# A two-layer transformer trunk on one core: weights repacked by the host, x also loaded transposed, and a first chunk that keeps the weights in the array

## The chip, the core and the metric

The kernel runs on one core of a Trainium2 chip. The metric is the device time of one launch in microseconds (us), the median of several runs. TensorE (PE) multiplies, VectorE (DVE) and ScalarE (ACT) do the elementwise work, GpSimd (POOL) a few small jobs, and SyncE (SP) issues all transfers (DMAs) in one queue, in program order.

## What is computed

The reference is a decoder trunk of two layers over 256 tokens of width 1024, in float32. Each layer is: half a SwiGLU feed-forward step, attention, a second half step, and a gated input embedding, each followed by a layer norm of `sqrt(2) * x + step`. Layer 0 has "forgetting" attention with 16 heads, layer 1 latent attention (MLA) with 16 heads.

```python
def swiglu(x, w_in, w_out):
    h = x @ w_in                                  # 1024 -> 2 * 2816
    gate, up = h[..., :D_FF], h[..., D_FF:]
    return (jax.nn.silu(gate) * up) @ w_out       # 2816 -> 1024

x = post_norm(x, 0.5 * swiglu(x, ffn1_w_in[i], ffn1_w_out[i]), ln_g[i, 0], ln_b[i, 0])
x = post_norm(x, mix, ln_g[i, 1], ln_b[i, 1])     # mix: FoX (i = 0) or MLA (i = 1)
x = post_norm(x, 0.5 * swiglu(x, ffn2_w_in[i], ffn2_w_out[i]), ln_g[i, 2], ln_b[i, 2])
gate = jax.nn.sigmoid(x @ ple_w_gate[i] + ple_b_gate[i])
x = post_norm(x, gate * (p[i] @ ple_w_proj[i]), ln_g[i, 3], ln_b[i, 3])
```

## The kernel before, in words

**Split products.** Every float32 operand of a matmul is split into two parts in a shorter format: `hi`, a copy rounded by ACT, and `lo = value - hi`, made by DVE (lines 194 and 195 for weights, 522 and 523 for activations). A product is three matmuls: hi·hi, hi·lo, lo·hi. So every weight passes from HBM into a `raw` buffer (1 MB, three of them), is split by ACT and DVE in *units* of 128 x 1024 into a slot of `hl` (ten slots, and up to four borrowed buffers called `ota`, `otb`, `qk`, `fs`), and is then used by TensorE.

**The stream.** `Stream` knows the order of all weights from a dry run. A *group* is one `raw` buffer, two units. `load` issues the next group's DMAs on SP as soon as the program has split an earlier group, so that at most three groups are in flight; SP then waits, in order, until the buffer's last reader is done. `pump`, which is called between matmuls, emits the split of the next unit if a small planner (`pe_t`, `act_t`, `dve_t`, `arrives`, with an assumed 4.2 us for a group) thinks that its data are there and that ACT and DVE are not far behind. The order of ACT, DVE and PE instructions is thus fixed when the program is built.

**The feed-forward step.** The 2816 hidden columns are worked through in 11 chunks of 256 (256 gate and 256 up columns each). `HT(c)` computes a chunk transposed: the weights are stationary (128 x 128), and `xT`, the split and transposed x, moves with its 256 tokens. That is 8 k-tiles x 4 column blocks x 3 products, 96 matmuls of 256 columns. `W` multiplies the chunk's result with its `w_out` rows.

**The first chunk of the program** (`first`, used with `cold=True` for ffn1 of layer 0) is different, as nothing has been loaded yet. x comes in eight DMAs of 128 KB (two token tiles by four column quarters), interleaved with sixteen 128 KB DMAs of the first two weight groups (`between`, lines 338 to 350, in `loads`; `fine` is 1 for these groups, 2 for the third and 4 from then on). `turn(t, q)` transposes two 128 x 128 tiles of x on TensorE (line 517) and splits the result into `xT`. `part(t, k, w)` then has x stationary and the weights moving: three matmuls of 512 columns for each token tile and k-tile, 48 in all. `act` forms `silu(gate) * up` for one token tile, and `T(0)`, later, transposes the result in four steps. Ahead of all this `setup` and `first` run `spin(2)` (line 493): two float32 matmuls of the all-zero `mask` each, whose results nobody reads. Between them `mask` gets its triangles from POOL (line 482).

Chunk 1 (`HT(1)`) follows at once with `T(0)` between its second and third unit, then chunks 2, 3 and 4 and their `W` steps.

Of the kernel before, what the change touches and what calls it, by code (L numbers as in the profile page):

```python
# [16 lines left out]
DFF = 2816  # L17
# [14 lines left out]
FINE = 4  # L32
# [59 lines left out]
class Recorder:  # L92
# [10 lines left out]
    lend = reclaim = check = load = busy = pair = split = ahead = later = split_now = fill = pump  # L103
# [3 lines left out]
class Stream:  # L107
# [66 lines left out]
    def split(self, between=lambda: None, half=False):  # L174
# [18 lines left out]
        def part(c):  # L193
            nc.scalar.activation(hi[:, c], src[:, c], AF.Copy)  # L194
            nc.vector.tensor_tensor(lo[:, c], src[:, c], hi[:, c].bitcast(F32), op=ALU.subtract)  # L195

        if self.ready < FINE:
            self.hl[key] = w
            part(slice(0, 1))
            between()  # L200
            part(slice(1, 2))
        elif key[0] == "pb":
            nc.gpsimd.memset(w[:, 0, :].bitcast(F32), 0.0)
            lo = w[32:33, 0, :n]
            part(slice(None))
        elif half:
            nc.scalar.activation(hi, src, AF.Copy)
            self.busy(act=n)

            def rest():  # L210
                nc.vector.tensor_tensor(lo, src, hi.bitcast(F32), op=ALU.subtract)
                self.busy(dve=n)
                self.split_done(key, w)

            self.rest = rest
            return
        else:
            part(slice(None))
# [113 lines left out]
def make_loads(a):  # L332
    def rows(ap, k0, n):
        return ap[k0 * 128 : (k0 + n) * 128, :].rearrange("(k p) c -> p k c", p=128)

    def loads(q, g, raw, fine, between):
        k, i = g[0], g[-1]
        if k == "win":
            w = a[g[2]][0][g[1]]
            c = g[3]  # L340
            r = raw.rearrange("p (k c) -> p k c", c=512)
            n = fine
            for k0 in range(0, 4, n):
                if n == 1 and (i, k0) in between:
                    between[i, k0]()
                for s in range(2):
                    c0 = DFF * s + 256 * c
                    q.dma_start(
                        r[:, k0 : k0 + n, 256 * s : 256 * s + 256], rows(w[:, c0 : c0 + 256], 4 * i + k0, n)
                    )  # L350
        elif k == "fv":
            w = a["fox_w_in"][0]
            q.dma_start(raw.rearrange("p (k c) -> p k c", c=512), rows(w[:, 2048:2560], 4 * i, 4))
        elif k == "fvb":
            w = a["fox_w_in"][0]
            q.dma_start(raw.rearrange("p (k c) -> p k c", c=256), rows(w[:, 2560:2816], 0, 8))
        elif k == "fvc":
            w = a["fox_w_in"][0]
            n = 6 - 4 * i
            q.dma_start(raw[:, 0 : 272 * n].rearrange("p (k c) -> p k c", c=272), rows(w[:, 2816:3088], 6 * i, n))  # L360
        elif k in ("fk", "fq"):
            w = a["fox_w_in"][0]
            c = (1024 if k == "fk" else 0) + 256 * i
            q.dma_start(raw.rearrange("p (k c) -> p k c", c=256), rows(w[:, c : c + 256], 0, 8))
        elif k in ("wout", "fo", "pg", "pp", "mo"):
            if k == "wout":
                w = a[g[2]][1][g[1]]
            elif k == "fo":
                w = a["fox_w_o"][0]
            elif k == "mo":  # L370
                w = a["mla_w_o"][0]
            elif k == "pg":
                w = a["ple_w_gate"][g[1]]
            else:
                w = a["ple_w_proj"][g[1]]
            q.dma_start(raw.rearrange("p (k c) -> p k c", c=1024), rows(w, 2 * i, 2))
        elif k == "pb":
            q.dma_start(raw[0:1, 0:1024], a["ple_b_gate"][g[1] : g[1] + 1, :])
        elif k == "kd":
            q.dma_start(raw[:, 0:1280].rearrange("p (k c) -> p k c", c=320), rows(a["kv_w_down"], 4 * i, 4))  # L380
        elif k == "dq":
            q.dma_start(raw[:, 0:1536].rearrange("p (k c) -> p k c", c=384), rows(a["mla_w_dq"][0], 4 * i, 4))
        elif k == "qr":
            w = a["mla_w_uq"][0]
            for s in range(2):
                kk = 2 * i + s
                if kk < 3:
                    q.dma_start(
                        raw[:, 1024 * s : 1024 * s + 1024].rearrange("p (h d) -> p h d", d=64),
                        w[128 * kk : 128 * kk + 128, :, 128:192],  # L390
                    )
        elif k == "kvv":
            w = a["kv_w_up"]
            for kk in range(2):
                q.dma_start(
                    raw[:, 512 * kk : 512 * kk + 512].rearrange("p (h d) -> p h d", d=128),
                    w[128 * kk : 128 * kk + 128, 4 * i : 4 * i + 4, 128:256],
                )
        elif k == "kq":
            for kk in range(5):  # L400
                w, r = (a["kv_w_up"], kk) if kk < 2 else (a["mla_w_uq"][0], kk - 2)
                q.dma_start(
                    raw[:, 256 * kk : 256 * kk + 256].rearrange("p (h d) -> p h d", d=128),
                    w[128 * r : 128 * r + 128, 2 * i : 2 * i + 2, 0:128],
                )
        else:
            raise KeyError(g)

    return loads
# [13 lines left out]
class Trunk:  # L423
# [33 lines left out]
    def setup(self):  # L457
# [18 lines left out]
        warm = self.tl([128, 1], F32, "ss", 2)  # L476
# [10 lines left out]
        self.S.lend("ota", "otb", "qk", "fs")  # L487
# [12 lines left out]
    def load_x(self, t, q):  # L500
        c = slice(256 * q, 256 * q + 256)
        self.dma(self.x[t][:, c], None if self.rec else self.a["x"][0, 128 * t : 128 * t + 128, c])


# [99 lines left out]

    def ffn(self, li, which, lni, kv=False, ple=False, at=None, cold=False):
# [12 lines left out]
        def first():  # L618

            ps = [self.bank("h") for _ in range(2)]  # L620

            def part(t, k, w):
                for i, j in SWEEPS[4][0]:
                    self.mm(
                        ps[t], self.xT[:, t, i, k, :], w[:, j, 512 * (k % 2) : 512 * (k % 2) + 512],
                        k == 0 and (i, j) == (0, 0), k == 7 and (i, j) == SWEEPS[4][0][-1],
                    )

            def turn(t, q):
                tr = self.bank("tr")  # L630
                c = slice(2 * q, 2 * q + 2)
                for i in range(2):
                    k = 2 * q + i
                    self.transpose(tr[:, 128 * i : 128 * i + 128], self.x[t][:, 128 * k : 128 * k + 128])
                self.parts(
                    self.xT[:, t, 0, c, :], self.xT[:, t, 1, c, :],
                    tr[:, 0:256].rearrange("p (k c) -> p k c", c=128),
                )

            S.hold = True  # L640
            turn(0, 0)
            self.spin(2)
            old = None
            for u in range(4):
                key = ("win", li, which, 0, u)

                def mid():
                    turn(1, u)
                    if u:
                        part(1, 2 * u - 1, old)  # L650
                    part(0, 2 * u, S.hl.get(key, Dummy()))

                S.split(mid)
                if self.rec:
                    mid()
                w = old = self.use(key)
                if u < 3:
                    turn(0, u + 1)
                else:
                    S.split()  # L660
                part(0, 2 * u + 1, w)
                if u == 3:
                    act(0, 0, ps[0])
                    S.split()
                part(1, 2 * u, w)
            S.split()
            part(1, 7, w)
            S.hold = False
            act(0, 1, ps[1])
# [21 lines left out]
        def HT(c, what=None):  # L691
            ring = "tr" if c % 2 == cold else "h"
            ps = [self.bank(ring) for _ in range(2)]
            for u in range(4):
                if u == 1 + (cold and c == 1) and what:
                    what()
                w = self.use(("win", li, which, c, u))
                for kk, b in ((kk, b) for kk in range(2) for b in range(4)):
# [6 lines left out]
                    )  # L705
            gt = self.tl([128, 768], F32, "P", 2)[:, 0:512]
# [35 lines left out]
        def spare(ring):  # L742
            tr = self.bank(ring)
            for k in range(4):
                self.transpose(tr[:, 128 * k : 128 * k + 128], self.ident)

        turns = (
            lambda: T(0, "h"),
            lambda: spare("h") if cold else T(1, "tr"),
# [869 lines left out]
```

## Time and profile before

| what | before |
|---|---|
| time, median of 3 runs | 1083.58 us (1083.28 to 1084.54) |
| profiled execution: span, first to last instruction | 1080.8 us |
| what lies around the span, against the median | 2.8 us |
| PE, DVE, ACT busy | 1065.8, 718.8, 543.3 us |
| read from HBM | 196.35 MB, 183 GB/s over the span |
| DMA packets | 151428, of which 130994 are under 2 KB and 11954 under 512 B |

The page gives no separate time for the profiled execution; its span and the median differ by the 2.8 us that lie around it, and this document takes these as they are. In the views a row such as `L513 PE MATMUL h<-hl,xT 128*128 128x512 f32 x48` means: line 513, TensorE, a matmul into tile `h` from `hl` and `xT`, 48 of them with 512 columns. The ends of matmuls are modelled, so the mean duration of a matmul is longer than the distance from one to the next; the chain of work that ended last shows the distance.

### The profile page before, as it was taken

The page shows a single profiled execution, that of the slowest core. Times are in us where ns is not written, and L with a number is a line of the kernel's source. Part 1 is how long each engine was busy: PE and PEld are TensorE (multiplying, and loading weights), DVE is VectorE, ACT ScalarE, POOL GpSimd, SP SyncE. Part 2 cuts the span into 40 slices and gives each one's busy share as a digit, 9 for nine tenths or more (in the row PEclk, how much of TensorE's full clock was granted, in tenths as well). Part 3 has the DMA queues.
Part 4 walks back from the last instruction along what each step waited for, and adds up shares of the span by engine and source line. Part 5 has one row for each costly group of instructions (what it writes and reads, how often), then busy time and mean ns, then how long its engine had stood idle before and what let it go on. Part 6 is the DMA issues. An engine that isn't in the chain of part 4 may idle for free.

```text
span 1080.8 us, 17731 instructions
## 1 busy us (share of the span) xinstructions
PE 1065.8 (99%) x7210; PEld 971.2 (90%) x7210; DVE 718.8 (67%) x1042; ACT 543.3 (50%) x806; POOL 73.2 (7%) x104
## 2 busy tenths in 40 slices
PE   9999999999999999999999999999999999999996
PEld 7989999899879999998899999988899889898986
DVE  4665645888797545558966564388777886455566
ACT  4565433666646444444555443336576465444431
POOL 0000000222200000000320000012200000000000
PEclk9999999999999999999999999999999999999999
DMA  8787752653358756455588564343445568565502
GB/s 270 230 312 241 245 181 83 195 166 137 114 172 290 254 181 190 148 201 156 164 275 266 185 194 165 89 105 112 140 145 169 174 225 308 191 206 192 182 13 78
DMA packets 151428, 198.54 MB, mean 184 GB/s; under 512 B 11954, under 2 KB 130994, under 8 KB 151348
## 3 DMA queue, kind: packets, MB, share of 16 engines
q1 hardware_dynamic: 151348, 197.43, 55.8%
q8 instruction: 56, 0.92, 0.3%
q14 instruction: 24, 0.20, 0.1%
HBM read 196.35 MB, written 1.05 MB: 183 GB/s over the span
## 4 chain that ended last, share of the span: by engine, by line
PE 90%; DVE 6%; issue 2%; ACT 2%; POOL 1%; DVEq 0%; POOLq 0%; ACTq 0%
PE y L513 32%; PE h L513 32%; PE tr L513 23%; PE tr L517 2%; DVE hl L195 2%; DVE x L593 1%; ACT hl L194 1%; DVE st L575 0%; DVE x L574 0%; PE h L517 0%; DVE PT L523 0%; ACT P L1460 0%; PE tr L1100 0%; DVE g L833 0%; POOL rs L585 0%
## 5 line engine op out<-in xcount | busy, mean ns | idle before, releaser
L195 DVE TENSOR_TENSOR hl<-raw,hl 128x1024 fp32r<-128x1024 f32 (+3 forms) x276 | 321.4, 1183 | 152.0 <-ACT hl L194 150.4
L194 ACT ACTIVATE hl<-raw 128x1024 fp32r<-128x1024 f32 (+3 forms) x276 | 274.4, 1016 | 187.0 <-PE y L513 95.0
L513 PE MATMUL y<-hl,g 128*128 128x512 f32 x816 | 190.7, 390 | 0.0
L513 PEld LDWEIGHTS y<-hl,g 128*128 128x128 f32 x816 | 152.0, 188 | 30.7
L513 PE MATMUL tr<-xT,hl 128*128 128x256 f32 x1512 | 177.3, 277 | 0.0
L513 PEld LDWEIGHTS tr<-xT,hl 128*128 128x128 f32 x1512 | 174.6, 188 | 0.9 <-DVE hl L195 0.2
L513 PE MATMUL h<-xT,hl 128*128 128x256 f32 x1464 | 174.0, 278 | 0.1
L513 PEld LDWEIGHTS h<-xT,hl 128*128 128x128 f32 x1464 | 170.0, 188 | 1.5 <-DVE qk L523 0.3
L513 PE MATMUL h<-hl,xT 128*128 128x512 f32 (+2 forms) x348 | 80.9, 379 | 0.5 <-DVE xT L523 0.4
L513 PEld LDWEIGHTS h<-hl,xT 128*128 128x128 f32 x348 | 61.5, 188 | 13.0 <-DVE xT L523 0.9
L513 PE MATMUL y<-hl,xT 128*128 128x512 f32 (+3 forms) x360 | 65.4, 334 | 0.0
L513 PEld LDWEIGHTS y<-hl,xT 128*128 128x128 f32 x360 | 55.5, 188 | 6.3 <-ACT xT L522 0.4
L585 POOL TENSOR_TENSOR rs<-ve,mhalf 128x1 f32<-128x1 f32 x16 | 15.2, 952 | 601.2 <-DVE ve L584 601.2
L522 ACT ACTIVATE xT<-tr 128x512 fp32r<-128x512 f32 (+1 forms) x36 | 19.2, 550 | 57.1 <-PE tr L517 57.0
L513 PE MATMUL y<-hl,otb 128*128 128x512 f32 x168 | 43.4, 399 | 0.7 <-DVE hl L195 0.5
L523 DVE TENSOR_TENSOR g<-P,g 128x512 fp32r<-128x512 f32 x37 | 25.6, 692 | 25.8 <-ACT g L522 25.8
L522 ACT ACTIVATE g<-P 128x512 fp32r<-128x512 f32 x37 | 23.4, 632 | 32.2 <-DVE P L708 32.2
L513 PEld LDWEIGHTS y<-hl,otb 128*128 128x128 f32 x168 | 30.2, 188 | 7.2 <-DVE hl L195 0.8
L195 DVE TENSOR_TENSOR otb<-raw,otb 128x1024 fp32r<-128x1024 f32 (+1 forms) x20 | 24.1, 1202 | 16.8 <-ACT otb L194 16.8
L195 DVE TENSOR_TENSOR qk<-raw,qk 128x1024 fp32r<-128x1024 f32 (+1 forms) x21 | 25.7, 1222 | 10.8 <-ACT qk L194 10.8
L707 ACT ACTIVATE P<-tr 128x512 f32<-128x512 f32 x20 | 12.0, 598 | 40.2 <-PE tr L513 40.2
L708 DVE TENSOR_TENSOR P<-P,tr 128x512 f32<-128x512 f32 x20 | 13.8, 688 | 26.8 <-PE tr L513 15.1
(259 smaller groups left out, 1411.6 us busy)
## 6 DMA issues: line engine op xcount, KB each, us to landing
raw<-in_ffn_w_in_dram SPq DMA_DIRECT2D x170, 512.0 KB, 4.8
raw<-in_ffn_w_out_dram SPq DMA_DIRECT2D x44, 1024.0 KB, 5.0
raw<-in_fox_w_in_dram SPq DMA_DIRECT2D x11, 1024.0 KB, 5.4
raw<-in_ple_w_gate_dram SPq DMA_DIRECT2D x8, 1024.0 KB, 5.1
raw<-in_mla_w_o_dram SPq DMA_DIRECT2D x8, 1024.0 KB, 5.0
gb<-in_ln_g_dram SPq DMA_DIRECT2D x8, 512.0 KB, 6.4
gb<-in_ln_b_dram SPq DMA_DIRECT2D x8, 512.0 KB, 7.8
raw<-in_fox_w_o_dram SPq DMA_DIRECT2D x4, 1024.0 KB, 4.9
```

Of the source, the lines that this page charges most:

```text
L194: nc.scalar.activation(hi[:, c], src[:, c], AF.Copy)
L195: nc.vector.tensor_tensor(lo[:, c], src[:, c], hi[:, c].bitcast(F32), op=ALU.subtract)
L513: self.nc.tensor.matmul(out, lhsT, rhs, start=start, stop=stop)
L517: self.nc.tensor.transpose(out, in_, self.ident)
L522: self.nc.scalar.activation(hi, src, AF.Copy)
L523: self.nc.vector.tensor_tensor(lo, src, hi.bitcast(F32), op=ALU.subtract)
L585: nc.gpsimd.tensor_tensor(rs, ve, self.mhalf, op=ALU.pow)
L593: nc.vector.scalar_tensor_tensor(xs, xs, rs if i else mv[:, 0:1], self.gb[:, i, c0:c1], op0=ALU.mult if i else ALU.subtract, op1=ALU.add i ...
L707: nc.scalar.activation(gt, ps[0], AF.Silu)
L708: nc.vector.tensor_tensor(gt, gt, ps[1], op=ALU.mult)
```

## The change

It has four parts, all in one edit.

1. The host packs every weight into the order of the `raw` buffers (`_packed`), so that each of the 128 partitions of a buffer reads one contiguous run (8 KB for a full group). A group is now one DMA where it was two for `w_in`, five for a `kq` group, two or four for others. The number of bytes of weights is unchanged.
2. The host also gives x transposed (`xt`). At the start SP issues, in this order: xt tile 0 (128 KB), weight k-tile 0 (256 KB), xt 1, weight 1, xt 2 and 3, weight 2, weight 3, xt 4 and 5, weight 4, weight 5, xt 6 and 7, weight 6, weight 7. x itself, which the first layer norm needs, is loaded by two 512 KB DMAs ahead of chunk 3. The transposed x lies in the borrowed buffer `fs` (`xraw`), which the stream gets as a slot only after the first chunk's splits.
3. The first chunk has the weights stationary, as `HT` has it: 96 matmuls of 256 columns. The splits of its four units are cut by `split_pieces` into k-tiles, the first into halves, and all are emitted ahead of the first matmul. Its `hi` of the first 256 columns is made by a DVE copy. `close` ends the chunk as it ends the others, so `T(0)` is gone.
4. The sixteen transposes of x are gone; `spin(1)` runs in `setup` and none in `first`, which begins with four transposes of the identity (`spare("tr")`).

```diff
@@ Stream
+    def split_pieces(self, key, todo):
+        src, _, n = unit_of(key, self.raw[group_of(key)])
+        slot = self.slots.pop(0)
...
+        for x in todo:
+            if callable(x):
+                x()
+                continue
+            what, k, c = x[0], x[1], slice(*x[2:])
+            if what == "both":
+                nc.scalar.activation(hi[:, k, c], src[:, k, c], AF.Copy)
+            if what == "hi":
+                nc.vector.tensor_copy(hi[:, k, c], src[:, k, c])
+            else:
+                nc.vector.tensor_tensor(lo[:, k, c], src[:, k, c], hi[:, k, c].bitcast(F32), op=ALU.subtract)
+        self.pair(n)
+        self.split_done(key, w)
@@ loads
         if k == "win":
-            for k0 in range(0, 4, n):
-                if n == 1 and (i, k0) in between:
-                    between[i, k0]()
-                for s in range(2):
-                    c0 = DFF * s + 256 * c
-                    q.dma_start(
-                        r[:, k0 : k0 + n, 256 * s : 256 * s + 256], rows(w[:, c0 : c0 + 256], 4 * i + k0, n)
-                    )
+            w = a[g[2]][0][g[1], g[3], i]
+            for k0 in range(0, 4, fine):
+                between.pop((i, k0), lambda: None)()
+                c = slice(512 * k0, 512 * (k0 + fine))
+                q.dma_start(raw[:, c], w[:, c])
+        elif k == "wout":
+            q.dma_start(raw, a[g[2]][1][g[1], i])
...
@@ setup
-        self.load_x(0, 0)
-        x = lambda t, q: lambda: self.load_x(t, q)
-        self.S.between = {
-            (0, 1): x(1, 0), (0, 2): x(0, 1), (0, 3): x(1, 1),
-            (1, 0): x(0, 2), (1, 1): x(1, 2), (1, 2): x(0, 3), (1, 3): x(1, 3),
-        }
+        self.xraw = self.tl([128, 8, 256], F32, "fs", 1)
+        self.load_xt(0, 1, nc.sync)
+        x = lambda *k: lambda: self.load_xt(*k, nc.sync)
+        self.S.between = {(0, 1): x(1, 2), (0, 2): x(2, 4), (1, 0): x(4, 6), (1, 2): x(6, 8)}
         self.S.load(2)
-        self.spin(2)
+        self.spin(1)
...
-        self.S.lend("ota", "otb", "qk", "fs")
+        self.S.lend("ota", "otb", "qk")
@@ ffn, first (the old body with turn, part, spin(2) and act is removed)
+            key = lambda u: ("win", li, which, 0, u)
+            def xs(k):
+                def f():
+                    self.parts(
+                        self.xT[:, :, 0, k, :], self.xT[:, :, 1, k, :],
+                        self.xraw[:, k, :].rearrange("p (t c) -> p t c", c=128),
                     )
+                return f
             S.hold = True
+            self.spare("tr")
             for u in range(4):
+                if u == 0:
+                    head = (("hi", 0, 0, 256), xs(0), ("lo", 0, 0, 256), ("both", 0, 256, 512))
                 else:
+                    head = (xs(2 * u), ("both", 0, 0, 512))
+                S.split_pieces(key(u), head + (xs(2 * u + 1), ("both", 1, 0, 512)))
+            S.lend("fs")
+            for u in range(4):
+                w = self.use(key(u))
+                for kk in range(2):
+                    k = 2 * u + kk
+                    for i, j in ((0, 0), (1, 0), (0, 1)):
+                        for b in range(4):
+                            self.mm(
+                                ps[b // 2][:, 256 * (b % 2) : 256 * (b % 2) + 256],
+                                w[:, j, 512 * kk + 128 * b : 512 * kk + 128 * b + 128], self.xT[:, :, i, k, :],
+                                (k, i, j, b % 2) == (0, 0, 0, 0), (k, j, b % 2) == (7, 1, 1),
+                            )
+                if u:
+                    S.split()
             S.hold = False
-            act(0, 1, ps[1])
+            close(0, ps)
...
         turns = (
-            lambda: T(0, "h"),
+            None if cold else lambda: T(0, "h"),
...
@@ run
-        self.ffn(0, "ffn1", 0, at={8: [keep("qk", "fs")]}, cold=True)
+        self.ffn(0, "ffn1", 0, at={3: [self.load_x], 8: [keep("qk", "fs")]}, cold=True)
@@ on the host
+    for n in ("ffn1", "ffn2"):
+        w = a[n + "_w_in"].reshape(2, 2, 4, 128, 2, NCH, 256)
+        o[n + "_in"] = w.transpose(0, 5, 1, 3, 2, 4, 6).reshape(2, NCH, 2, 128, 2048)
...
+    o["xt"] = a["x"][0].T.reshape(8, 128, 256).transpose(1, 0, 2)
```

In the last loop `i` names the part of x and `j` the part of the weight (0 is hi): the four hi·hi matmuls of a k-tile come first, then the four with x's lo, then the four with the weight's lo.

More of the change, by code (lines that the diff above doesn't have):

```diff
@@ L101, in pump @@
         pass
-    lend = reclaim = check = load = busy = pair = split = ahead = later = split_now = fill = pump
+    lend = reclaim = check = load = busy = pair = split = split_pieces = ahead = later = split_now = fill = pump
     between, hl, hold = {}, {}, False
@@ L172, in later, with split @@
             f()
-    def split(self, between=lambda: None, half=False):
+    def split(self, half=False):
         self.later()
@@ L217, in split @@
         else:
-            part(slice(None))
+            both()
+        self.pair(n)
+        self.split_done(key, w)
+    def split_pieces(self, key, todo):
+        nc = self.nc
+        assert key == self.order[self.ready]
+        src, _, n = unit_of(key, self.raw[group_of(key)])
+        slot = self.slots.pop(0)
+        self.slot_of[key] = slot
+        w = self.pool.tile([128, 2, 1024], F32R, tag=slot, name=slot, bufs=1)
+        hi, lo = (w[:, i, :].rearrange("p (a b) -> p a b", b=512) for i in range(2))
+        for x in todo:
[9 more added lines that the diff above has]
+                nc.vector.tensor_tensor(lo[:, k, c], src[:, k, c], hi[:, k, c].bitcast(F32), op=ALU.subtract)
         self.pair(n)
@@ L406, in loads @@
+        elif k in ("kd", "dq", "kvv", "kq"):
+            w = a[k][i]
+            q.dma_start(raw[:, 0 : w.shape[1]], w)
         else:
@@ L602, in ln, with spare @@
         self.ln_apply(t, st, eps)
+    def spare(self, ring):
+        tr = self.bank(ring)
+        for k in range(4):
+            self.transpose(tr[:, 128 * k : 128 * k + 128], self.ident)
     def ffn(self, li, which, lni, kv=False, ple=False, at=None, cold=False):
@@ L694, in HT @@
             for u in range(4):
-                if u == 1 + (cold and c == 1) and what:
+                if u == 1 and what:
                     what()
```

180 lines of the change are left out of this document (57 added, 123 removed).

## The prediction, made before the changed kernel was run

> **What bounds the kernel now.** I read the page's busy shares first, then the chain of work that ended last, then that chain in order of time for the first 60 us.
>
> ```profile
> span 1080.8 us, 17731 instructions
> PE 1065.8 (99%) x7210; PEld 971.2 (90%) x7210; DVE 718.8 (67%) x1042; ACT 543.3 (50%) x806; POOL 73.2 (7%) x104
> PE 90%; DVE 6%; issue 2%; ACT 2%; POOL 1%; DVEq 0%; POOLq 0%; ACTq 0%
> ```
>
> TensorE is the bound nearly everywhere. No DMA stands on the chain, so repacked weights as such can give nothing back once the stream runs. What is idle lies in few places:
>
> ```profile
> 740.00:760.00 20.00, 16.51 (x116) 14.56 (x115) 16.71 (x33) 11.48 (x25) 10.82 (x9) 1.00 0.28 86
> 1070.00:1081.00 11.00, 2.64 (x24) 2.45 (x22) 7.26 (x18) 0.61 (x2) 0.92 (x1) 0.81 0.20 72
> ```
>
> The first number after the stretch is its length, the next PE's busy time: 3.5 us of idle PE in MLA, with DVE at 16.7 of 20 us, and 8.4 us in the last norm. The change touches neither. What it touches is the start:
>
> ```profile
> 1.70 2.48 issue
> ...
> 4.21 0.55 POOL mask L482 x2
> ...
> 4.80 1.65 PE y L493 x4
> 6.45 0.23 PE tr L517 x2
> ...
> 9.79 1.37 PE h L513 x6
> ...
> 20.06 5.50 PE tr L513 x46
> 25.55 0.44 PE h L517 x4
> 25.99 5.67 PE tr L513 x48
> 31.66 10.88 PE h L513 x96
> ```
>
> Until 6.45 us the chain is the spins (L493) and the mask between them, not data. Then comes the first chunk, and chunk 1 ends at 31.66. That is my yardstick: from there the kernels do the same PE work in the same order. Six matmuls of 512 columns take 1.37 us, so the first chunk's 48 are 10.96; chunk 1's 96 of 256 columns are 10.88 (last row, same form); sixteen transposes of x at 0.23 for two are 1.8; T(0) is 0.44. Work 24.1 us; so **7.6 us** of the 31.66 are start, spins and waits.
>
> **The change part by part.**
>
> *Work removed.* The first chunk's 96 matmuls of the new form cost 10.88 by the last row above, against 10.96: nothing. The 48 more weight loads are hidden, as chunk 1 has the same 96 in the same time. Transposes and T(0): minus 2.2 us.
>
> *First data.* The first rows are SP's issues; the last is the time from issue to landing of the two first weight DMAs.
>
> ```profile
> 0.74 0.40 SPq L445 DMA_DIRECT2D x<-in_x_dram  x1
> 1.19 0.90 SPq L348 DMA_DIRECT2D raw<-in_ffn_w_in_dram  x2
> 10.66 0.43 SPq L445 DMA_DIRECT2D x<-in_x_dram  x1
> DMA to landing us min/median/max: 2.2/2.2/2.2
> ```
>
> The new first weight DMA also goes out at 1.19 but carries 256 KB, 0.5 us more at the 253 GB/s below: it lands at about 3.9. The DVE copy of 256 columns is not in the trace; the nearest rows are these:
>
> ```profile
> L195 DVE TENSOR_TENSOR hl<-raw,hl 128x512 fp32r<-128x512 f32 x8 | 5.5, 691 | 0.7
> L194 ACT ACTIVATE hl<-raw 128x512 fp32r<-128x512 f32 x8 | 5.0, 622 | 0.0
> L523 DVE TENSOR_TENSOR xT<-tr,xT 128x256 fp32r<-128x256 f32 x8 | 3.4, 424 | 8.5 <-ACT xT L522 8.5
> L522 ACT ACTIVATE xT<-tr 128x256 fp32r<-128x256 f32 x8 | 3.1, 385 | 7.7 <-PE tr L517 7.7
> ```
>
> Bounds 0.17 (half of 0.35, what 691/2 gives) and 0.42; I take 0.4, the row of its size. The first matmul is then at **4.35 us** against 6.45. x's hi is ready by 3.6 (ACT, 385 ns after a landing near 3.2), so it is not last.
>
> *Pace of the splits.* A k-tile costs ACT 0.385 + 0.622 = 1.0 and DVE 0.424 + 0.691 = 1.1 us; PE takes 10.88 / 8 = 1.36. So PE is behind the splits from the second k-tile on. In the first, DVE makes x's lo, then two weight halves after the copy, 3 x 0.42: the last lo is there at 4.3 + 1.3 = 5.6, where PE would want it at 5.35 (two thirds and a half of a third of 1.36 after 4.35). I charge 0.2. Undisturbed, the chunk ends at 4.35 + 10.88 + 0.2 = **15.4**.
>
> *The clock.* The loads ahead of the spin's equal matmuls lie 0.65 us apart early and 0.32 later:
>
> ```profile
> 2.00 0.34 PEld L493 LDWEIGHTS y<-mask 128*128 128x128 f32 x1 [0.30 <-issue]
> 2.65 0.34 PEld L493 LDWEIGHTS y<-mask 128*128 128x128 f32 x1 [0.30 <-issue]
> ...
> 5.32 0.19 PEld L493 LDWEIGHTS y<-mask 128*128 128x128 f32 x1
> 5.64 0.19 PEld L493 LDWEIGHTS y<-mask 128*128 128x128 f32 x1
> ```
>
> So TensorE starts at half speed and is at full speed by about 5.2 (the first matmul of the second spin still takes 4.80 to 5.32), though the granted-clock column says 1.00 throughout. Before, the slow time fell on spins. Now one spin (two half matmuls, 1.2 to 2.6) and four transposes end near 3.5, PE idles to 4.35, and real matmuls may run slow. If full speed still comes near 5.5, that costs half of the 1.15 us, **0.6**. Bounds: 0 (full speed at 4.35) and 2.0 (the rival below).
>
> *Supply.* All 13 DMAs of x and two groups, 3.15 MB, are issued at 0.45 us each, by about 6.7; before, the 24 were issued until 12 us, so SP set the pace: 128 KB in 0.47 us. The rates of the three stretches:
>
> ```profile
> 2.00:12.00 10.00, 9.67 (x37) 6.19 (x36) 4.44 (x9) 4.41 (x12) 0.69 (x3) 1.00 0.83 253
> 12.00:17.00 5.00, 5.00 (x27) 4.02 (x26) 3.53 (x7) 2.89 (x7) 0.00 (x0) 1.00 0.94 264
> 18.00:27.00 9.00, 8.98 (x71) 8.48 (x71) 4.59 (x6) 4.38 (x7) 0.00 (x0) 1.00 1.03 345
> 17.69 1.06 ACT L194 ACTIVATE hl<-raw 128x1024 fp32r<-128x1024 f32 x1 [0.54 <-DMA raw<-in_ffn_w_in_dram]
> 22.33 1.06 ACT L194 ACTIVATE hl<-raw 128x1024 fp32r<-128x1024 f32 x1 [2.25 <-DMA raw<-in_ffn_w_in_dram]
> ```
>
> Last column GB/s, before it the share of the DMA engines. The last two rows say that chunk 1's weights, split at 17.69 and 22.33, waited for their DMA even before: **when PE starts earlier, supply is what is late next.** I take 300 to 345 GB/s, between the rows, for DMAs of twice the size. Chunk 1's first unit needs 3.15 + 0.52 = 3.67 MB: from 2.0 us, 12.2 us at 300 or 10.6 at 345, 1 us until landing, then 1.06 (ACT) and 1.22 (DVE): 17.5 or 15.9. PE, at 15.4 + 0.6 = 16.0, meets that unit's lo in its third matmul. I charge **0.7**, between 0 and 1.5. The later units have 2.7 us of PE each against 1.5 to 1.75 us of transfer, so they catch up.
>
> *Moved and hidden.* x's own two DMAs (1 MB, 3 us at 345 GB/s) stand on SP's queue ahead of chunk 3's later loads, behind those which wait for a buffer. They delay the stream by 3 us in this stretch, where the DMA engines are at 0.59 and PE is never idle:
>
> ```profile
> 40.00:50.00 10.00, 10.00 (x91) 10.00 (x90) 6.39 (x7) 6.92 (x8) 0.00 (x0) 1.00 0.59 181
> ```
>
> Their reader is the norm near 190 us. Without that cover it would be 3 us of PE. The mask's triangles wait for one spin, not two, and then nothing waits for them. One DMA in place of two to five, the late slot `fs`, and the two norm inputs: nothing, under PE's 99%.
>
> *The sum.* Chunk 1 ends at 15.4 + 0.6 + 0.7 + 10.9 = 27.6 against 31.66: **4.1 us** saved. The profiled execution would span 1080.8 - 4.1 = 1076.7; with the 2.8 us around it, **1079.5** against 1083.58.
>
> **The rivals.**
>
> *Supply keeps its old pace* (the new order does not bring the data sooner). At 253 GB/s to the end of the second group and 345 after it, 3.15 MB end at 14.4, the next half group at 15.9, is landed and split at 19.2; chunk 1 ends at 30.0: 1.7 saved, **1081.9**; at 264 GB/s 1081.4. For it: 12 to 17 us shows 0.94 of the engines busy at only 264. Against it: those were 128 KB DMAs, and the rate rose to 345 when larger ones followed.
>
> *The clock opens late.* If the transposes do nothing to open it and the idle stretch after them undoes the spin, the count starts again at 4.35. Before, full speed came 4.0 us after the first matmul (1.20 to 5.2); now it would come at 8.35, and half of 4.0, **2.0 us**, is lost. That hides the supply wait, as PE meets chunk 1's first unit at 17.4: 15.4 + 2.0 + 10.9 = 28.3, 3.4 saved, **1080.2**. For it: the spin is half as long and the idle stretch, 3.5 to 4.35, is longer than the 0.6 us that PE's loads stood before the second spin. Against it: before, the clock opened across such a gap. The Trainium skill, "TensorE: Matmul & The Clock Gate", Part 4, states that transpose mode does not count as busy for the clock gate; by that rule this rival is the likelier one. Its Part 1 has a window of about 3.4 us that runs freely, so that a start at 4.35 would open between 7.8 and 11.2 and lose 1.7 to 3.4 (an estimate from that page). No row here separates transposes from the spin.
>
> *All goes well*: clock open by 4.6, no supply wait; chunk 1 ends at 26.3, 5.4 saved, **1078.2**.
>
> *Slower: the splits are planned into worse places.* The planner's PE clock is some 1.2 us smaller after the first chunk (sixteen transposes less, four added), so that its tests on arrivals and slack can move splits far behind. A unit's split put ahead of urgent DVE work costs PE between 0 and 1.06 + 1.22 = 2.3 us; the place is MLA between 740 and 760 us, where PE stood 3.5 us already. To be slower than before by 0.2% needs 4.1 + 2.2 = 6.3 us, four displaced splits at 1.6: then **1085.8**. For it: DVE is the near bound there. Against it: by then a slot decides when a split is made, not the arrivals, and MLA's order is written out.
>
> **How the numbers follow.** The forecast, 1078.7 to 1079.9, has 0.50; the late clock, 1079.9 to 1081, 0.20; supply's old pace, 1081.2 to 1082, 0.15; all well 0.10; slower 0.05. A measurement of this kernel tells about 0.2% (2.2 us) from no change, so "faster" is below 1081.4: the forecast, all well, the late clock and a third of the slow supply, 0.85; "same" is the rest of it, 0.10; slower 0.05. The range is 1077.2 to 1082.0: down to all well with 1 us for bounds I set too high, up to the slow supply.
>
> **What would show it.** In the chain, the first matmul of line 513's kind at 4.2 to 4.5 us, and the first chunk's 96 ending near 16; no transposes of x. Matmuls of 256 columns 0.22 us apart after 4.35 show the slow clock, and for how long. DMA from 2 to 12 us above 290 GB/s shows the supply right; ACT rows of chunk 1 that wait for DMA longer than 2 us show it wrong. A changed difference after 60 us, at 740 to 760 above all, would show the plan at work and make the prediction wrong.

## The result and the profile after

| | before | after |
|---|---|---|
| time, median | 1083.58 us | 1081.13 us (1079.73 to 1083.5) |
| ratio, 95% interval | | 0.9976 (0.9965 to 0.9987) |
| span of the profiled execution | 1080.8 us | 1079.2 us, with a time of 1081.13 |
| end of chunk 1 | 31.66 us | 30.09 us |

The change saves 2.45 us in the median, where 4.1 were forecast: faster, with the whole interval of the ratio below 1, inside the range, at six tenths of the size. The page of the changed kernel, as far as it differs:

```profile
span 1079.2 us, 17531 instructions
PE 1061.9 (98%) x7236; PEld 971.8 (90%) x7236; DVE 719.3 (67%) x1043; ACT 543.3 (50%) x805; POOL 73.1 (7%) x104
DMA packets 32947, 199.58 MB, mean 185 GB/s; under 512 B 3682, under 2 KB 5218, under 8 KB 12004
PE 90%; DVE 6%; ACT 2%; issue 1%; POOL 1%; DMA 0%; DVEq 0%; SPq 0%; POOLq 0%; ACTq 0%
```

The packets fell from 151428 to 32947, and the chain's shares stayed: PE 90%, DVE 6%. The gain is at the start. The chain in order of time (start, length, what):

```profile
0.74 0.39 SPq L468
...
1.18 4.63 DMA raw<-in_ffn_in_dram
...
5.84 0.42 ACT hl L231
...
6.28 12.93 PE h L482 x96
19.21 10.88 PE tr L482 x96
30.09 10.88 PE h L482 x96
```

Where the chain before ran over spins and POOL's mask, it now starts with one DMA, the first weights: issued at 1.18, landed at 5.8. The first matmul is at 6.28, only 0.14 before the first one of before (6.42). The 96 matmuls of the first chunk take 12.93 us, 2.05 more than the 96 of chunk 1 right behind them. Chunk 1 ends 1.57 us sooner than before, and the spans differ by 1.6: in this pair of profiles the whole gain is made by then.

The medians differ by more, by 2.45 us. Two things lie between. The profiled execution of before is one of its faster ones: its span is 1080.8 us, where the 79 executions of that kernel beside the experiments have median spans of 1081.9 to 1082.4; the 1079.2 us after are the median of seven. And what lies around the span is 2.1 to 2.2 us in each of those 79 executions and 1.8 to 1.9 us in the seven of the changed kernel, so some 0.3 us are gained outside the span; why stays open, as e3_hold, a variant of the changed kernel, has 2.1 to 2.2 us again. The 2.8 us that the table of before and the prediction use are the median of some executions less the span of another.

In this profile MLA's weak stretch is what it was (16.51 us of PE in 20 there before, too):

```profile
740.00:760.00 20.00, 16.51 (x116) 14.62 (x116) 16.17 (x33) 10.98 (x28) 12.34 (x10) 1.00 0.30 93
```

Why 12.93? TensorE's weight loads in two stretches (start, length, count):

```profile
6.25 3.27 PEld L482 LDWEIGHTS h<-xT,hl 128*128 128x128 f32 x15 [2.95 <-ACT hl L231]
10.32 2.79 PEld L482 LDWEIGHTS h<-xT,hl 128*128 128x128 f32 x24
```

The single loads start 0.213 us apart in the first stretch and 0.113 in the second. The array ran at half speed until about 10 us, as the granted clock in the profile, 1.00 throughout this stretch, does not show. What the DMAs moved, in GB/s, is the last column here, with the share of the DMA engines before it:

```profile
2.00:7.00 5.00, 2.42 (x9) 1.64 (x8) 1.16 (x4) 1.52 (x6) 0.68 (x3) 1.00 0.90 230
7.00:12.00 5.00, 5.00 (x33) 5.00 (x32) 3.47 (x8) 3.40 (x8) 0.00 (x0) 1.00 1.01 326
12.00:17.00 5.00, 5.00 (x46) 5.00 (x45) 3.60 (x7) 3.42 (x8) 0.00 (x0) 1.00 1.02 396
```

From 12 to 17 us it is 396 GB/s where it was 264; in the first five, 230, no better than before.

### The profile page after: what moved, and what is told of

The parts are those of the page before. It is cut to its first block, busy times and chain, and to the rows that moved or that the text cites. A ratio compares the mean times of both kernels' runs of the same rounds, so it can differ in the third digit from the quotient of the medians.

```text
span 1079.2 us, 17531 instructions
## 1 busy us (share of the span) xinstructions
PE 1061.9 (98%) x7236; PEld 971.8 (90%) x7236; DVE 719.3 (67%) x1043; ACT 543.3 (50%) x805; POOL 73.1 (7%) x104
## 2 busy tenths in 40 slices
DMA packets 32947, 199.58 MB, mean 185 GB/s; under 512 B 3682, under 2 KB 5218, under 8 KB 12004
## 4 chain that ended last, share of the span: by engine, by line
PE 90%; DVE 6%; ACT 2%; issue 1%; POOL 1%; DMA 0%; DVEq 0%; SPq 0%; POOLq 0%; ACTq 0%
PE y L482 32%; PE h L482 32%; PE tr L482 22%; DVE hl L194 2%; PE tr L486 2%; DVE x L562 1%; ACT hl L193 1%; DVE st L544 0%; DMA raw<-in_ffn_in_dram 0%; DVE x L543 0%; PE h L486 0%; ACT P L1418 0%; DVE PT L492 0%; PE tr L1058 0%; DVE g L791 0%
## 5 line engine op out<-in xcount | busy, mean ns | idle before, releaser
L194 DVE TENSOR_TENSOR hl<-raw,hl 128x1024 fp32r<-128x1024 f32 (+3 forms) x268 | 316.1, 1198 | 149.1 <-ACT hl L193 148.2
L193 ACT ACTIVATE hl<-raw 128x1024 fp32r<-128x1024 f32 (+3 forms) x268 | 269.8, 1028 | 183.5 <-PE y L482 96.7
L482 PE MATMUL h<-xT,hl 128*128 128x256 f32 x1560 | 186.8, 279 | 3.0 <-ACT hl L231 2.6
L482 PEld LDWEIGHTS h<-xT,hl 128*128 128x128 f32 x1560 | 182.7, 190 | 4.8 <-ACT hl L231 2.9
L482 PE MATMUL h<-hl,xT 128*128 128x512 f32 (+2 forms) x300 | 67.8, 374 | 0.4 <-DVE xT L492 0.4
L482 PEld LDWEIGHTS h<-hl,xT 128*128 128x128 f32 x300 | 53.2, 188 | 10.7 <-DVE xT L492 0.9
L491 ACT ACTIVATE xT<-tr 128x512 fp32r<-128x512 f32 x28 | 16.1, 596 | 49.4 <-PE tr L486 49.3
L194 DVE TENSOR_TENSOR qk<-raw,qk 128x1024 fp32r<-128x1024 f32 (+1 forms) x21 | 25.7, 1222 | 11.5 <-ACT qk L193 11.4
```

The source lines that it names most:

```text
L482: self.nc.tensor.matmul(out, lhsT, rhs, start=start, stop=stop)
L491: self.nc.scalar.activation(hi, src, AF.Copy)
```

## The experiments

My theory after the result: the first chunk is late for two reasons, the landing of the first weights (1.9 us later than forecast) and a clock that opens only while the first chunk runs (1.7 us lost); the packing itself gives nothing. The rivals: the splits pace the first chunk; a 256 KB DMA is slow by itself; the packing gains elsewhere. All ratios below are against runs of the kernel before on the same chip, in three groups: e1 to e4 (1084.02 us for the kernel before), e5 to e8 (1084.39) and e9 to e11 (1084.54).

### Two spins ahead of the first chunk (e1_spin)

```diff
             self.spare("tr")
+            self.spin(2)
```

> The changed kernel with two more zero matmuls (spin) between the four identity transposes and the first chunk. Theory: the first chunk's 96 matmuls take 12.9 us instead of 10.9 because TensorE's clock is slow for the first 3.5 us of them. Then here full speed comes before 6.3 us, the 96 matmuls take 11.0 to 11.4 us at 0.113 apart from the start, chunk 1 ends 1.5 to 1.8 us earlier (28.3 to 28.6), the time is 1079.3 to 1079.7, and the runs spread less than the 3.8 us of the changed kernel. Rival: the splits pace the first chunk; then it stays at 12.9 us and the time at 1081.1.

Measured: 1080.94 us, ratio 0.9968 (0.9956 to 0.9981). Its chain and weight loads:

```profile
3.07 5.30 DMA raw<-in_ffn_in_dram
...
8.39 7.17 DMA raw<-in_ffn_in_dram
...
17.95 10.94 PE tr L482 x94
28.89 10.88 PE h L482 x96
```

```profile
5.67 11.86 PE L482 MATMUL h<-xT,hl 128*128 128x256 f32 x96
6.09 2.02 PEld L482 LDWEIGHTS h<-xT,hl 128*128 128x128 f32 x17 [0.16 <-issue]
```

From 6.09 the loads lie 0.114 us apart: the clock is open, and the slow chunk is gone, so the splits were not its pace. The 96 matmuls still take 11.86 us, not 11.0 to 11.4, as they wait for weights: the chain now runs through DMAs again, through the third k-tile's weights, which landed at 8.37, then through chunk 1's first unit, split at 17.9. Chunk 1 ends at 28.89, not at 28.3 to 28.6: 1.2 us sooner than in the first profile, less than the 1.7 that the clock cost there, though the first weights landed sooner here. Supply takes the rest back, and the time is not the 1079.3 to 1079.7 expected.

### Twelve more transposes instead (e2_transposes)

```diff
             self.spare("tr")
+            for _ in range(3):
+                self.spare("tr")
```

> As the run with two spins, but the stretch is filled with twelve more identity transposes (to about 6 us) in place of the spins. Theory: transposes do not open the clock (as the Trainium skill states in TensorE: Matmul & The Clock Gate, Part 4): the first chunk stays at 12.6 to 13.0 us with matmuls 0.21 apart until about 9.8, time 1081. Rival: any work of the array opens it, and only the idle 2.8 us ahead of the first matmul kept it shut; then 11.0 to 11.4 us and 1079.5, as with the spins.

Measured: 1080.64 us, ratio 0.9964 (0.9952 to 0.9977). I had expected a first chunk as slow as in the changed kernel; the loads of the transposes say why it is not:

```profile
2.64 1.08 PEld L486 LDWEIGHTS tr<-ident 128*128 128x128 f32 x5 [0.41 <-issue]
...
4.23 0.80 PEld L486 LDWEIGHTS tr<-ident 128*128 128x128 f32 x7
```

They start 0.21 us apart and end 0.11 apart: the clock opened near 4.2, in the middle of them. The spin at 1.2 to 2.6 came first, however, so this run alone can't say what opened it.

### Transposes alone, no spin (e5_only_transposes)

```diff
-        self.spin(1)
...
-            self.spare("tr")
+            for _ in range(5):
+                self.spare("tr")
```

> The changed kernel with no spin at all and twenty identity transposes ahead of the first chunk (1.7 to about 5.5 us). Theory, revised after the run with twelve more transposes, whose clock opened near 4.2: transposes open the clock as matmuls do, so it opens between 4 and 6 us, the transposes go from 0.21 to 0.11 us apart, and no more than a few of the first chunk's matmuls are 0.21 apart; time 1080 to 1081. Rival (the Trainium skill, TensorE: Matmul & The Clock Gate, Part 4): transposes do not count, the spin opened the clock in that run; then it opens only 3 to 4 us after the first matmul, at 9 to 10 us, the first chunk takes 12.5 us or more, and the time is that of the changed kernel, 1081 to 1082.

Measured: 1081.57 us, ratio 0.9977 (0.9968 to 0.9986).

```profile
1.82 3.85 PEld L485 LDWEIGHTS tr<-ident 128*128 128x128 f32 x18
...
6.44 2.48 PEld L481 LDWEIGHTS h<-xT,hl 128*128 128x128 f32 x21
```

Eighteen transposes at 0.213, and the first chunk's matmuls at 0.114 or 0.118 from 6.44 on, half a microsecond after the first of them. But for three loads of the first chunk, only transposes had run before. So transposes open the clock, some 4.6 us after the first. The Trainium skill, "TensorE: Matmul & The Clock Gate", Part 4, states that transpose mode does not count as busy for the gate; for this kernel's float32 transposes of the identity, which the profile lists as MATMUL, the measurement says otherwise. The chunk nevertheless took 11.47 us, as its matmuls from the third k-tile on lie 0.118 us apart, a distance told of at the end. The time lies in the rival's 1081 to 1082, not in the 1080 to 1081 expected; with executions from 1079.67 to 1083.03 us it does not tell the two theories apart, the trace does.

### The first weights alone in flight (e3_hold)

```diff
-                between.pop((i, k0), lambda: None)()
+                between.pop((i, k0), lambda r: None)(raw)
...
+        def held(r):
+            if not self.rec:
+                nc.vector.tensor_copy(self.xraw[:, 1, 0:1], r[:, 0:1])
+            self.load_xt(1, 2, nc.sync)
...
-        self.S.between = {(0, 1): x(1, 2), ...
+        self.S.between = {(0, 1): held, ...
```

> The changed kernel, but SP's second DMA of xt, and so all DMAs behind it, waits until the first weight DMA has landed (a copy of one column by DVE stands between). Theory: that first DMA of 256 KB lands late (4.6 us after its issue, at 5.8) because the DMAs issued behind it share the 16 engines with it; alone it lands 2.2 to 2.8 us after issue, at 3.4 to 4.0, and the first matmul starts at 3.9 to 4.5. The second k-tile then comes late, so the time gains nothing (1081 to 1084). Rival: a 256 KB DMA with 2 KB runs needs its 4.6 us by itself; then it still lands at 5.8, the first matmul stays at 6.3, and all is 3 to 4 us later (1084 to 1085).

Measured: 1085.56 us, ratio 1.0013 (1.0003 to 1.0023), above both forecasts.

```profile
1.18 3.17 DMA raw<-in_ffn_in_dram
4.35 0.02 issue
4.37 0.04 DVE fs L443
...
4.92 4.54 DMA raw<-in_ffn_in_dram
...
10.16 11.44 PE h L488 x84
```

With nothing behind them, the 256 KB land 3.2 us after their issue, a little later than the theory had it, against 2.2 for the two 128 KB DMAs of before and 4.6 in the changed kernel's profile. Both theories have a part: by these profiles twice the size costs 1.0 us, and the DMAs behind it 0.2 to 1.5 more. How much more differs from run to run: the same order of DMAs gave 3.4, 3.5, 3.6, 3.8, 3.9, 4.0 and 4.6 us in the seven profiles that have it. The forecast of 2.7 was below all of them.

### The packing alone (e4_packed)

```diff
-                        r[:, k0 : k0 + n, 256 * s : 256 * s + 256], rows(w[:, c0 : c0 + 256], 4 * i + k0, n)
+            if fine == 4:
+                q.dma_start(raw, w)
+                return
...
+                    q.dma_start(r[:, k0 : k0 + fine, c], w[:, k0 : k0 + fine, c])
```

The kernel before, its start included, with the packed weights as its source; every group from the fourth on is one DMA, as in the change, and the third comes in four pieces.

> The kernel before with the packed weights alone: its own start, with the same x loads and 128 KB pieces of the first two groups, and every later group in one contiguous DMA. Theory: no DMA is on the chain, so the packing gives nothing: 1083.0 to 1084.2, chunk 1 ends at 31.5 to 31.8, and nothing differs behind it. Rival: the packing is what gains (fewer and longer DMAs land earlier or disturb less); then it takes 1081 to 1082 with an unchanged start.

Measured: 1084.6 us, ratio 1.0002 (0.9993 to 1.0011): no difference, with a median a little above the 1083.0 to 1084.2 expected. The packing by itself gives nothing that these runs can tell from zero. In the profile chunk 1 ends at 32.26 us, not at 31.5 to 31.8: the clock opened at 6.2 us where it had opened at 5.1, and most matmuls of 256 columns lay 0.118 us apart. The clock's opening differs by more between e2_transposes and e10_fill, which are one kernel, and the distance is told of at the end; nothing here lays either to the packing.

### Fewer and larger first DMAs (e6_large)

```diff
+            0: [(0, 512), x(1, 4), (512, 1024), (1024, 2048)],
+            1: [x(4, 8), (0, 1024), (1024, 2048)],
```

The pairs are columns of the weight group (512 are one k-tile), `x(a, b)` the transposed x from tile a to b. Twelve more transposes stand ahead of the chunk here.

> The changed kernel with twelve more transposes and the first 3.15 MB in 8 DMAs in place of 13: xt 0, weight 0, xt 1 to 3, weight 1, weights 2 and 3 together, xt 4 to 7, weights 4 and 5, weights 6 and 7. Theory: with the clock open, supply is what is late, and the early rate (230 GB/s from 2 to 7 us) suffers from the number of DMAs; fewer give 270 GB/s or more there, but each lands later, so the second and third k-tile wait 0.5 to 1.5 us: time within 0.7 us of the run with twelve more transposes. Rival: the number of DMAs does not matter for the early rate; it stays at 225 to 245 and the time is 1 us or more above that run.

Measured: 1081.8 us, ratio 0.9978 (0.9969 to 0.9986). The rate from 2 to 7 us stayed at 233 GB/s, as the rival had it; from 7 to 12 it was 394. The median is 1.2 us above that of the run with twelve more transposes, which ran on another chip. The second k-tile's weights now stand behind a DMA of 384 KB:

```profile
8.49 1.44 PEld L486 LDWEIGHTS h<-xT,hl 128*128 128x128 f32 x12 [0.66 <-ACT hl L231]
10.31 8.25 PEld L486 LDWEIGHTS h<-xT,hl 128*128 128x128 f32 x72 [0.37 <-ACT hl L231]
```

TensorE waited before the second and the third k-tile, and had one clear run of 72 behind them.

### Small first DMAs, large later ones (e7_halves)

```diff
+            0: [(0, 256), (256, 512), x(1, 2), (512, 768), (768, 1024), x(2, 4), (1024, 1536), (1536, 2048)],
+            1: [x(4, 8), (0, 1024), (1024, 2048)],
```

Eight more transposes here. The edit loads weights 2 and 3 as two DMAs, where the expectation speaks of one.

> Eight more transposes, and the first DMAs small and the later ones large: weights 0 and 1 as halves of 128 KB (the first chunk needs one half for its first eight matmuls), then xt 2 and 3, weights 2 and 3 together, xt 4 to 7, weights 4 and 5, weights 6 and 7. Theory: a small DMA lands sooner and SP's 0.45 us for each keeps fewer of them in flight, so the first half lands 2.2 to 2.8 us after its issue, near 3.8, the first matmul starts at 4.2 to 4.8, and chunk 1 ends at 28.0 to 28.8, time 1079.3 to 1080.3. Rival: the data as a whole come no sooner; the first matmul starts earlier but the third k-tile or chunk 1's first unit waits as long, and chunk 1 ends at 28.9 to 29.3 as in the runs with spins or transposes (1080.6 to 1081).

Measured: 1084.07 us, ratio 1.0002 (0.9993 to 1.0011): the whole gain is gone, which neither forecast had.

```profile
9.58 1.45 PEld L486 LDWEIGHTS h<-xT,hl 128*128 128x128 f32 x12 [0.72 <-ACT hl L231]
12.24 1.45 PEld L486 LDWEIGHTS h<-xT,hl 128*128 128x128 f32 x12 [1.21 <-ACT hl L231]
14.92 5.71 PEld L486 LDWEIGHTS h<-xT,hl 128*128 128x128 f32 x48 [1.24 <-ACT hl L231]
```

The first half did land 2.4 us after its issue, as expected. But the third, fourth and fifth k-tile waited for their weights, which SP now issues two DMAs later and with larger ones behind: those of the fourth landed 7.0 us after their issue. The clock opened only at 7.2 us, with the first k-tile nearly done, and chunk 1 ends at 32.17. The edit changes several DMAs at once, so it does not say which of them does the harm. The lesson: with PE earlier, what ends last is the later weights.

### The changed kernel again, with and without the filled gap (e8_same, e11_same, e10_fill, e9_single)

e8_same and e11_same are the changed kernel without an edit, e10_fill is e2_transposes again, and e9_single has, on top of it, xt 2 and xt 3 as two DMAs:

```diff
-        self.S.between = {(0, 1): x(1, 2), (0, 2): x(2, 4), (1, 0): ...
+        self.S.between = {(0, 1): x(1, 2), (0, 2): x(2, 3), (0, 3): x(3, 4), (1, 0): ...
```

> The changed kernel itself, run on the same chip beside the others. Both theories: 2 to 3 us below the kernel before; the first matmul between 5.4 and 6.4, the clock opening 3 to 4 us after it, chunk 1 ending at 29.5 to 30.3 if its matmuls are 0.113 apart, 0.9 later if they are 0.118 apart, as they were in the profiles of two earlier runs.

> The changed kernel again, as the partner of the other two. Both theories: 2.0 to 2.8 us below the kernel before; first chunk's end 18.6 to 19.3.

> The changed kernel with twelve more transposes, a second time, now beside the changed kernel on the same chip. Theory: the clock opens before or with the first matmul, the first chunk then waits for weights, and the chunk ends at 17.3 to 18.0 in place of 18.7 to 19.2: 0.8 to 1.5 us faster than the changed kernel in the median. Rival: the supply takes back all of it; within 0.4 us of the changed kernel.

> The changed kernel with twelve more transposes and xt 2 and xt 3 as two DMAs of 128 KB, the second behind weight 2. Theory: with the clock open the first chunk is paced by the landing of its weights, the third k-tile above all; 128 KB less ahead of weight 2 lets it land about 0.4 us sooner, the first chunk ends 0.2 to 0.4 us sooner than in the run beside it without this, and the time is 0 to 0.5 us lower. Rival: landing depends on all that is in flight, not on what stands ahead in the queue; then the third k-tile lands when it did and the time is the same or, with one DMA more, higher.

Measured: e8_same 1082.23 us, ratio 0.9985 (0.9976 to 0.9994); on another chip e11_same 1081.79, 0.9977 (0.9968 to 0.9985); beside it e10_fill 1080.9, 0.9972 (0.9961 to 0.9982), and e9_single 1080.64, 0.9968 (0.9957 to 0.9979). The chain and the weight loads of e8_same:

```profile
1.19 3.46 DMA raw<-in_ffn_in_dram
...
5.12 13.57 PE h L482 x96
18.69 10.88 PE tr L482 x96
```

```profile
5.25 4.82 PEld L482 LDWEIGHTS h<-xT,hl 128*128 128x128 f32 x22
```

Here the first weights landed at 4.65 and the first matmul was at 5.12, 1.2 us sooner than in the first profile; yet the 96 matmuls took 13.57 us, with 22 loads 0.213 apart, and ended only 0.5 us sooner. e11_same is the same (5.21, then 13.62). The first matmul came earlier than the 5.4 to 6.4 expected, and the clock opened later behind it, 5.2 us instead of 3 to 4. By the distance of the loads it opens at 10.1 to 10.5 us in the three profiles of the changed kernel, and between 4.1 and 7.2 us in the seven with a filled gap. So the two delays are not independent: weights that land sooner meet the slow clock for longer.

Not all of the lead lasts. At chunk 1's end e8_same is 2.09 us ahead of the kernel before and e11_same 1.95; at the end of the span it is 0.9 and 0.8. The rest is lost in MLA between 757 and 762 us. The changed kernel's first profile, then e8_same (the clock granted to TensorE is the third number from the end):

```profile
759.00:761.00 2.00, 1.91 (x11) 1.27 (x10) 1.01 (x4) 1.99 (x6) 1.58 (x2) 1.00 0.87 266
```

```profile
759.00:761.00 2.00, 2.00 (x8) 1.61 (x7) 1.54 (x5) 2.00 (x5) 1.01 (x1) 0.50 0.77 324
```

For about 3.4 us TensorE gets half its clock, which costs 1.15 us there, and here the granted clock shows it. e6_large and e10_fill have the same loss, the other nine profiles do not. It is not the plan of the splits: the first profile, e8_same and e11_same are one kernel, and so are e2_transposes, without the loss, and e10_fill. By an estimate it befalls the kernel before as well: 3.4 us at half clock lower the mean clock of 1080 us by 0.0016, and means of 0.996 in place of 0.998 stand beside 16 of 79 executions of before and 9 of 29 of the changed kernel. Whether the change makes it likelier is open.

e10_fill against e11_same is 0.9 us in the median, at the lower end of what was expected; the intervals overlap. Its clock opened at 6.8, after its first few matmuls. Its chunk 1 goes on at 18.10, with 94 matmuls to come, where e11_same starts its 96 at 18.84:

```profile
8.58 7.12 DMA raw<-in_ffn_in_dram
...
18.10 10.95 PE tr L482 x94
```

Between stands the wait for chunk 1's first unit. e9_single moves a wait once more. The third k-tile's weights, split by ACT in both, e9_single first and e10_fill second:

```profile
8.21 0.63 ACT L231 ACTIVATE hl<-raw 128x512 fp32r<-128x512 f32 x1 [0.25 <-DMA raw<-in_ffn_in_dram]
```

```profile
8.59 0.63 ACT L231 ACTIVATE hl<-raw 128x512 fp32r<-128x512 f32 x1 [0.22 <-DMA raw<-in_ffn_in_dram]
```

They came 0.4 us sooner, as the theory said; its first chunk ended sooner, but then chunk 1's first unit was late and its 94 matmuls started at 18.60. By its medians the version with the gap filled is the fastest seen (0.9964 and 0.9972 against before), with the split xt no different from it in time. But e10_fill's interval overlaps that of the changed kernel beside it: that filling the gap gains is seen in the chain, where chunk 1 ends at 29.05 against 29.71, and is not shown by the times.

## Why the prediction was right, and where its sizes were not

**The sign and the place** were right: in the first profile the gain lies ahead of chunk 1's end (1.57 of 1.6 us of span), and the packing, the extra loads of x, the late slot and the planner changed nothing behind it. e4_packed shows the packing's zero; for the others the equal stretch at 740 us and the equal differences at 30 and at 1080 us show it. The changed difference at 757 us in e8_same and e11_same, which the prediction would have taken for the plan at work, is the half clock told of above. Some 0.3 us of the gain lie outside the span, where the prediction had nothing change.

**Work removed** was right: no transposes of x, no T(0), and the new form costs the same per chunk (10.88 us at full clock).

**First data** is the first step that failed. Put at 3.9 us for the first weights' landing and 4.35 for the first matmul, it was 5.82 and 6.28 in the profile, 4.65 and 5.12 in e8_same. I had scaled a row of 128 KB by a mean rate; e3_hold shows 3.2 us for 256 KB alone, and the rest comes with the DMAs that SP puts behind it at once. DVE's copy, bounded at 0.17 to 0.42 us, took 0.29; what ends last by the chain is ACT's copy of the next 256 columns, 0.42, so that the step from landing to matmul, 0.46 us, was still sized right.

**The clock** is the second, and a rival was right here: charged at 0.6 us, it cost about 1.7 in the profile (some 17 matmuls at 0.213 in place of 0.113) and about 2.4 in e8_same (some 23). The late clock, priced at 2.0 with a chance of 0.20, happened in every profile of the changed kernel; its assumed mechanism did not hold in one half. The transposes do help to open the clock (e5_only_transposes); what undoes it is, as far as the runs show, the idle stretch behind them, 1.8 to 3.0 us instead of my 0.85. With that stretch the clock opens 3.9 to 5.3 us after the first load of the first chunk, which is within what it takes from a standing start (2.9 to 6.0 us after TensorE's first load, in the runs with the stretch filled); with the stretch filled it opens 3 to 6 us sooner. No run separates the length of the gap from the length of the work ahead of it. The stretch is so long because the first weights are late: one mis-sized term fed the next.

**Supply**, charged at 0.7 us for chunk 1's first unit, cost nothing there in the changed kernel, since the slow clock hid it; in four runs with an open clock (e1_spin, e2_transposes, e9_single, e10_fill) it stands on the chain, as the forecast had it, with 0.4 to 1.0 us. The rate over 2 to 12 us was 278 GB/s in the first profile (230 at first, then 326) and 292 and 296 in e8_same and e11_same, on both sides of the 290 named as the test; no split of chunk 1 waited longer than 1.4 us for its DMA.

**The sum** in the profile: 6.28 + 12.93 + 10.88 = 30.09, where the forecast had 4.35 + 11.68 + 0.7 + 10.88 = 27.6: 1.93 from the landing, 1.25 from the first chunk, less 0.7 of supply. One slip is inside the 0.2 charged for the pace of the splits: by its own terms PE wants the last lo at 5.48, not at 5.35, so it should have been 0.1.

**The number** lies in the range partly by luck. 1081.13 lies in none of the windows that got a chance: above the forecast's (to 1079.9) and the late clock's (to 1081), below the slow supply's (from 1081.2). The range held it only because it reached up to the slow supply, and the supply's old pace was not what happened: from 7 to 17 us it was 326 and 396 GB/s. "Faster" was close as well: on two other chips the same kernel took 0.9985 and 0.9977 of the time before, on either side of the 0.2% that the prediction could tell from no change.

## What to carry to other kernels

At a start, ask for each load when it has landed with everything behind it in flight, not when it would land alone: here that was 3.4 to 4.6 us against 3.2. Keep the array busy, with transposes if nothing else, right up to the first real matmul, and size that filler by the landing. Compare medians with medians and spans with spans of many executions: one pair of profiles showed 1.6 us where the medians had 2.45. And when one delay at the start goes, price the next one before counting the gain: here landing, clock and supply each hid a part of the others.

## What the runs showed of the hardware beside this

**The same matmuls have two distances.** Two 256-column chunks at the same place with an open clock, first e5_only_transposes, then the changed kernel's profile:

```profile
40.59 11.31 PE tr L481 x96
```

```profile
40.97 10.88 PE tr L482 x96
```

0.118 us against 0.113, with the granted clock at 1.00 in both. In e3_hold, e4_packed and e7_halves the slower distance held, but for short stretches, through the chunks up to the `W` steps near 67 us and was gone behind them; in e5_only_transposes it held from 9 until near 124 us, on both sides of those steps; in e9_single, of these stretches, it held only from about 93 to 124 us. It changed where other matmuls lay between, or where TensorE had waited, as in e5_only_transposes at 9.0 us. It costs 0.43 us for each chunk, some 1.2 to 3.1 us in such a run, as much as the whole change, and falls on kernels with either start. Executions of one kernel differ by 3 us here, and this may be a part of it, as the half clock in MLA is; but no kernel has a profile with the slower distance and another without it, so that is not shown. What decides it stays open.

**The early rate.** From 2 to 7 us the DMA engines are busy for 0.72 to 0.90 and move 220 to 256 GB/s whatever the DMAs are (128 to 512 KB, runs of 1 to 4 KB), in all kernels but e3_hold, which holds them back; from 12 to 17 us the same engines move 377 to 409 with the new start and 264 and 271 with the small DMAs of the old one. In these runs the larger DMAs pay only behind 7 us, and the first chunk waits for what comes before.
